# A two-layer hybrid decoder trunk: the engines' order laid out against another machine model

## Chip, core and metric
The kernel runs on one core of a Trainium2 chip. The metric is the device time of one execution in microseconds; the time given is the median of three runs. A profiled execution of the same program gives the rows below.

## The reference, cut to what matters
Two layers, each with a token mixer, a cross-attention and a feed-forward block, every one between two RMSNorms. All data is fp32; x is 512 x 1024.

```python
for l in range(DEPTH):                                   # DEPTH = 2
    a = hybrid_mixer(rms_norm(x, pre_mix_g[l]), positions, rel_bias, w_in[l], ...)
    x = x + rms_norm(a, post_mix_g[l])
    c = memory_cross_attention(rms_norm(x, pre_xattn_g[l]), rms_norm(mem, mem_g[l]), ...)
    x = x + rms_norm(c, post_xattn_g[l])
    hdn = square(relu(rms_norm(x, pre_mlp_g[l]) @ w_up[l]))
    x = x + rms_norm(hdn @ w_down[l], post_mlp_g[l])
# hybrid_mixer: z = h @ w_in is split into latent columns (8 heads of latent attention, causal,
# keys and queries through low-rank w_ukv and w_uq with rotary columns) and q, k, v of 8 dilated
# heads (three dilations with a shared relative bias, merged by their softmax denominators);
# both groups side by side @ w_mix_out
```

## The kernel before
The kernel is written in a tile framework: the source calls engine operations on tiles from pools, and the framework works out the waits, the buffers and the order of each engine's stream. Rows of x lie in four tiles of 128 tokens.

Every large product is made of three fp32r matmuls. A weight chunk `raw` (two blocks of 128 rows by up to 512 columns, loaded by SP, 8 buffers) is split into `whi` by ACT (L142, L162 or L167, the last with the norm's gain) and `wlo = raw - whi` by DVE (L143, L163, L172), 5 buffers each; x and other left sides are split likewise (L176 and L178). `mm` (L204 to L213) then adds high x low, low x high and high x high into one PSUM bank. `tok_major_steps` and `feat_major_steps` run such products with tokens or features on the partitions and write the PSUM tiles `ptm` and `pfm`.

The mixer is the one stage with two strands. `attention()` goes through 16 heads, first the eight dilated ones, then the eight latent ones. For each: the score matmuls `sp` (L432, two PSUM banks), DVE's `tensor_tensor_reduce` (L436), which adds the bias or mask table, writes `P` and the row's extreme `nm`, ACT's exponential (L438), DVE's reciprocal (L439), POOL's scaling (L440), the transposes `ptp` (L198) with their copies `PT` by ACT (L459) or DVE (L457), and for every two heads the product with the values `op` (L202). A dilated head takes a table `tb` of bias and log counts of its own, loaded by SP (L640). The other strand, `latent()` and `memory()`, are the latent projections and the keys and values of the cross-attention; `weave` calls steps of it between steps of attention, by a ratio of the PE time that both strands take by a count in the source:

```python
weave(attention(), [latent_gen, memory()], lambda: RATIOS[0] if not scored[0] else RATIOS[1])
```

A norm (`norm_x`) takes ACT's squares `junk` (L344), DVE's mean `n1m` (L348), POOL's power `n1r` (L124), POOL's scaled rows `xn` (L375) and eight PE transposes `tp` (L198). At the end of a feed-forward block `done` (sum of squares, product with the gain, L994) and `add_post_norm` (`pnr`, `xs`, L387 to L390) come before it. The feed-forward block makes `w_down`'s product from seven sub-products per quarter (L1020 to L1049); the partial sums are added into `acc` on DVE (L1047, L1049).

The order of the streams: the source gives a sequence for all engines together. On leaving the `with` block at L1093 the framework plays the program against a model of the machine. Each instruction that the model holds to be ready, with its buffer free, is taken in the order of the source; one that isn't ready is passed by. What comes out is the order that each engine then keeps on the chip: the queues of PE, DVE, ACT, POOL and SP are run in order. All 384 DMAs are issued by SP.

## Time and profile before
| | |
|---|---|
| median of three runs | 1551.03 us (1550.02 to 1554.45) |
| profiled execution | 1552.36 us, its span 1550.6 us |
| mean granted TensorE clock | 0.992 |
| PE busy | 1504.3 us, 97% of the span |
| PE weight loads (PEld) | 1263.1 us, 81% |
| DVE busy | 993.8 us, 64% |
| ACT busy | 819.0 us, 53% |
| POOL busy | 240.7 us, 16% |

The span runs from the first to the last instruction. The granted clock is a share of full speed, 2.4 GHz; the lower level is 1.2 GHz. On the time axis the first mixer's two-strand part lies at about 86 to 265 us, the first feed-forward block at about 500 to 773, the second layer's mixer at about 851 to 1030 and its feed-forward block at about 1270 to 1540. Idle time is told with what ended it; a wait of a matmul counts where PE had nothing else in its queue.

### The profile page before, as it was taken

The numbers are of one execution on the slowest core, as the hardware profiler recorded it, in microseconds if no ns is written. First come the engines' busy times: TensorE is split into PE (matmuls) and PEld (weight loads), VectorE is DVE, ScalarE is ACT, GpSimd is POOL, SyncE is SP. The second block draws the span as 40 slices with busy tenths as digits, with TensorE's granted clock in tenths as the row PEclk, the third lists the DMA queues.
The fourth block names the chain that finished last, engine by engine and source line by source line (L and its number), as shares of the span: only waits on it lengthen the run. The fifth ranks groups of instructions, "written<-read, shape, count | busy, mean of one in ns | idle before, by whom it ended". The sixth has DMA issues, their size and how long they took to land.

```text
span 1550.6 us, 21224 instructions
## 1 busy us (share of the span) xinstructions
PE 1504.3 (97%) x7831; PEld 1263.1 (81%) x7831; DVE 993.8 (64%) x1775; ACT 819.0 (53%) x1574; POOL 240.7 (16%) x433
## 2 busy tenths in 40 slices
PE   7999999999999999999999899999999999999997
PEld 5777788898898888888778877878988988888885
DVE  4655766456458677686954558663654595867678
ACT  5455766345356364545644557653553654636363
POOL 2033621021020000000022346211120200000000
PEclk9999999999999999999999999999999999999998
DMA  6432223514131505151631322234322325060522
GB/s 225 153 116 68 89 69 102 197 55 123 55 109 55 176 28 185 33 176 42 219 106 49 115 75 96 69 123 163 107 71 77 113 60 173 14 190 21 184 69 81
DMA packets 87403, 164.07 MB, mean 106 GB/s; under 512 B 6230, under 2 KB 12036, under 8 KB 87300
## 3 DMA queue, kind: packets, MB, share of 16 engines
q1 hardware_dynamic: 87300, 162.73, 32.7%
q8 instruction: 61, 1.00, 0.3%
q14 instruction: 42, 0.34, 0.1%
HBM read 154.29 MB, written 11.03 MB: 107 GB/s over the span
## 4 chain that ended last, share of the span: by engine, by line
PE 83%; DVE 7%; issue 4%; ACT 2%; POOL 2%; DMA 2%; SPq 0%; DVEq 0%; POOLq 0%; ACTq 0%
PE pfm L212 12%; PE pfm L211 12%; PE pfm L213 12%; PE ptm L211 6%; PE ptm L212 6%; PE ptm L213 6%; PE wa L211 3%; PE wa L212 3%; PE wa L213 3%; PE sp L432 3%; PE op L202 3%; DVE wlo L172 2%; PE ptp L198 2%; PE wc L211 2%; PE wc L212 2%
## 5 line engine op out<-in xcount | busy, mean ns | idle before, releaser
L212 PE MATMUL pfm<-xth,wlo 128*128 128x512 f32 (+1 forms) x896 | 322.4, 360 | 0.6
L211 PE MATMUL pfm<-xtl,whi 128*128 128x512 f32 (+1 forms) x896 | 322.2, 360 | 0.0
L213 PE MATMUL pfm<-xth,whi 128*128 128x512 f32 (+1 forms) x896 | 321.6, 359 | 0.0
L172 DVE SCALAR_TENSOR_TENSOR wlo<-raw,gT,whi 128x512 fp32r<-128x512 f32 (+3 forms) x332 | 229.5, 731 | 132.7 <-ACT whi L167 131.1
L167 ACT ACTIVATE whi<-raw,gT 128x512 fp32r<-128x512 f32 (+2 forms) x324 | 208.9, 697 | 177.8 <-PE pfm L213 92.7
L142 ACT ACTIVATE whi<-raw 128x1024 fp32r<-128x1024 f32 x112 | 118.9, 1061 | 139.8 <-PE pfm L213 52.8
L212 PEld LDWEIGHTS pfm<-xth,wlo 128*128 128x128 f32 x896 | 169.3, 189 | 26.9 <-DVE wlo L172 1.4
L213 PEld LDWEIGHTS pfm<-xth,whi 128*128 128x128 f32 x896 | 169.2, 189 | 25.6 <-issue 0.5
L211 PEld LDWEIGHTS pfm<-xtl,whi 128*128 128x128 f32 x896 | 169.3, 189 | 24.8
L143 DVE TENSOR_TENSOR wlo<-raw,whi 128x1024 fp32r<-128x1024 f32 x112 | 134.8, 1220 | 32.0 <-ACT whi L142 32.0
L124 POOL TENSOR_TENSOR pnr<-pnm,mhalf 128x1 f32<-128x1 f32 x24 | 16.1, 672 | 828.3 <-DVE pnm L387 828.3
L211 PE MATMUL wa<-wlo,fh 128*128 128x512 f32 x256 | 99.8, 390 | 0.5 <-DVE acc L1047 0.5
L212 PE MATMUL wa<-whi,fl 128*128 128x512 f32 x256 | 99.6, 389 | 0.0
L213 PE MATMUL wa<-whi,fh 128*128 128x512 f32 x256 | 99.6, 389 | 0.0
L440 POOL TENSOR_SCALAR P<-P,rs 128x128 f32<-128x128 f32 (+3 forms) x128 | 71.1, 560 | 152.3 <-DVE rs L439 79.3
L438 ACT ACTIVATE P<-P,nm 128x128 f32<-128x128 f32 (+3 forms) x128 | 71.1, 557 | 32.9 <-DVE nm L436 32.1
L163 DVE TENSOR_TENSOR wlo<-raw,whi 128x1024 fp32r<-128x1024 f32 x32 | 39.1, 1223 | 59.3 <-ACT whi L162 58.6
L211 PE MATMUL ptm<-wlo,xth 128*128 128x512 f32 (+2 forms) x192 | 69.4, 362 | 1.8 <-ACT xth L176 1.8
L162 ACT ACTIVATE whi<-raw 128x1024 fp32r<-128x1024 f32 x32 | 34.0, 1061 | 67.3 <-PE ptm L213 64.5
L212 PE MATMUL ptm<-whi,xtl 128*128 128x512 f32 (+2 forms) x192 | 68.5, 357 | 0.4 <-DVE xtl L178 0.4
L213 PE MATMUL ptm<-whi,xth 128*128 128x512 f32 (+2 forms) x192 | 67.2, 350 | 0.0
L211 PEld LDWEIGHTS wa<-wlo,fh 128*128 128x128 f32 x256 | 48.0, 188 | 11.3 <-DVE acc L1047 1.4
(244 smaller groups left out, 3254.0 us busy)
## 6 DMA issues: line engine op xcount, KB each, us to landing
raw<-in_w_up SPq DMA_DIRECT2D x64, 512.0 KB, 4.7
raw<-in_w_down SPq DMA_DIRECT2D x64, 512.0 KB, 4.4
raw<-in_w_in SPq DMA_DIRECT2D x24, 512.0 KB, 7.0
raw<-in_w_xk SPq DMA_DIRECT2D x16, 512.0 KB, 4.2
raw<-in_w_xv SPq DMA_DIRECT2D x16, 512.0 KB, 3.8
raw<-in_w_mix_out SPq DMA_DIRECT2D x16, 512.0 KB, 4.2
raw<-in_w_xq SPq DMA_DIRECT2D x16, 512.0 KB, 6.0
raw<-in_w_xo SPq DMA_DIRECT2D x16, 512.0 KB, 3.6
```

Source lines behind the costliest of these rows:

```text
L142: nc.scalar.activation(hi, raw, AF.Copy)
L143: nc.vector.tensor_sub(lo, raw, hi.bitcast(F32))
L163: nc.vector.tensor_sub(lo[:, :kts, :width], raw[:, :kts, :width], hi[:, :kts, :width].bitcast(F32))
L167: nc.scalar.activation(cols(hi, k, False), cols(raw, k, True), AF.Copy, scale=g)
L172: nc.vector.scalar_tensor_tensor(lv, rv, g, hv, op0=OP.mult, op1=OP.subtract)
L202: nc.tensor.matmul(ps, lhsT=lhsT, rhs=rhs, start=start, stop=stop)
L211: nc.tensor.matmul(ps, lhsT=lh, rhs=rl, start=first, stop=False, skip_group_check=more)
L212: nc.tensor.matmul(ps, lhsT=ll, rhs=rh, start=False, stop=False, skip_group_check=more)
L213: nc.tensor.matmul(ps, lhsT=lh, rhs=rh, start=False, stop=last, skip_group_check=more)
L432: nc.tensor.matmul(sp[:, :L], lhsT=q[:, i * 128:(i + 1) * 128], rhs=k[:, :L], start=n == 0, stop=n == len(parts) - 1)
L438: nc.scalar.activation(Pi, Pi, AF.Exp, bias=nm[:, i:i + 1], scale=-1.0, accum_out=rs[:, i:i + 1])
L440: nc.gpsimd.tensor_scalar(Pi, Pi, rs[:, i:i + 1], 1.0, op0=OP.mult, op1=OP.mult)
```

## The change
One argument of the framework's context is set, so that the model against which the order is laid out is another one of the framework's, a simulator of the timeline that has its own prices for operations, waits and transfers. The source of the work is the same.

```diff
-    with tile.TileContext(nc) as tc:
+    with tile.TileContext(nc, schedule_with_timeline_sim=True) as tc:
         block_kernel(tc, *args, o)
```

## Rows read from the trace of the kernel before

**Rows 1.** The page's first part: busy us (share of the span), instructions.
```profile
PE 1504.3 (97%) x7831; PEld 1263.1 (81%) x7831; DVE 993.8 (64%) x1775; ACT 819.0 (53%) x1574; POOL 240.7 (16%) x433
```

**Rows 2.** Busy time by stretch (columns in the first line).
```profile
core 0: us, PE busy (x) PEld busy (x) DVE busy (x) ACT busy (x) POOL busy (x), PEclk, DMA share, GB/s
0.00:30.00 30.00, 20.07 (x84) 15.05 (x84) 13.52 (x23) 16.50 (x35) 10.19 (x21) 1.00 0.82 290
...
90.00:110.00 20.00, 17.26 (x103) 14.28 (x102) 8.80 (x28) 11.23 (x29) 2.91 (x6) 0.91 0.41 135
...
140.00:150.00 10.00, 7.09 (x43) 4.72 (x41) 7.09 (x22) 6.39 (x17) 3.12 (x5) 1.00 0.67 231
150.00:200.00 50.00, 47.23 (x284) 38.16 (x283) 39.95 (x115) 34.33 (x88) 33.63 (x66) 1.00 0.25 79
...
500.00:770.00 270.00, 269.75 (x1190) 223.03 (x1190) 200.26 (x256) 141.49 (x204) 0.00 (x0) 1.00 0.38 121
770.00:800.00 30.00, 24.38 (x111) 18.40 (x110) 20.19 (x38) 14.91 (x35) 13.09 (x16) 0.94 0.42 133
...
850.00:870.00 20.00, 17.90 (x115) 16.68 (x115) 11.42 (x42) 10.93 (x33) 7.58 (x13) 0.91 0.32 107
870.00:900.00 30.00, 28.09 (x173) 24.28 (x171) 15.92 (x52) 16.11 (x45) 8.95 (x21) 0.94 0.28 88
900.00:915.00 15.00, 11.82 (x63) 10.19 (x62) 9.98 (x27) 9.52 (x21) 4.19 (x13) 0.89 0.53 175
915.00:965.00 50.00, 47.18 (x283) 38.07 (x282) 38.77 (x112) 33.63 (x87) 33.57 (x66) 1.00 0.25 80
...
1540.00:1551.00 11.00, 0.15 (x1) 0.00 (x0) 6.39 (x12) 1.34 (x4) 1.48 (x2) 0.60 0.42 157
```

**Rows 3.** Waits of PE: who waited for whom, us in total, times, longest.
```profile
PE sp L432 <- DVE nm L436: 12.2, 11, 2.0
PE tp L198 <- POOL xn L375: 10.8, 6, 4.9
...
PE ptp L198 <- ACT PT L459: 2.3, 4, 0.8
```

**Rows 4.** Timeline, 84 to 102 us: start, us, engine, what, [idle before <-releaser].
```profile
88.25 0.28 PE L432 MATMUL sp<-kh,qs 128*128 128x256 f32 x1
...
97.43 3.15 ACT L167 ACTIVATE whi<-raw,gT 128x384 fp32r<-128x384 f32 x6 [8.49 <-issue]
...
98.08 1.15 DVE L172 SCALAR_TENSOR_TENSOR wlo<-raw,gT,whi 128x384 fp32r<-128x384 f32 x2 [8.28 <-ACT whi L167]
...
101.22 0.28 DVE L436 CUSTOM_DVE_ANT_0 P<-sp,tb 128x128 f32<-128x128 f32 x1
```

**Rows 5.** Timeline of SP's queue, 825 to 890 us.
```profile
832.21 18.15 SPq L135 DMA_DIRECT2D raw<-in_w_uq  x2
...
852.21 0.41 SPq L640 DMA_DIRECT2D tb<-tabw  x1
```

**Rows 6.** Timeline, 855.9 to 859.2 us.
```profile
856.10 0.30 PE L212 MATMUL ptm<-whi,xtl 128*128 128x288 f32 x1
858.09 0.29 DVE L436 CUSTOM_DVE_ANT_0 P<-sp,tb 128x128 f32<-128x128 f32 x1 [2.64 <-DMA tb<-tabw]
...
858.44 0.44 PE L432 MATMUL sp<-kh,qs 128*128 128x384 f32 x1 [2.04 <-DVE nm L436]
```

**Rows 7.** Timeline of DVE, 764 to 796 us.
```profile
773.32 0.69 DVE L1049 TENSOR_TENSOR acc<-wa,acc 128x512 f32<-128x512 f32 x1
773.92 0.15 DVE L348 SCALAR_TENSOR_TENSOR n1m<-n1ms 128x1 f32<-128x1 f32 x1
```

**Rows 8.** All on the tile tb: DVE's waits for it, issue to landing.
```profile
  DMA tb<-tabw: 10.7, 4
...
DMA to landing us min/median/max: 2.6/4.6/6.0
```

## Prediction

> **What bounds the kernel now.** I read the page's busy times first, then the busy time by stretch, then who waits for whom on PE, then the timelines around PE's largest stops. PE is the bound: 1504.3 us of 1550.6 are busy, while DVE has 64% and ACT 53% [rows 1]. So the time is PE's own work, which this change leaves as it is, plus PE's stops, 46.3 us, plus what PE loses at the lower of its two clock levels (1.2 instead of 2.4 GHz).
>
> Where the 46.3 us lie is read from the stretches [rows 2]: 9.9 in the first 30 us, where the first rows of x and the first weights are on their way; 10.9 behind the last matmul, where the last norm and the stores run; 5.6 between the layers (770 to 800 us); and in the two mixers 18.4, as 2.74 + 2.91 + 2.77 in the first and 2.10 + 1.91 + 3.18 + 2.82 in the second. In a feed-forward stage PE is busy for 269.75 of 270 us. Those stages have nothing to gain.
>
> A stop costs more than itself. In five of the stretches with such stops the granted clock reads 0.89 to 0.94 and not 1.00 [rows 2]. Length times what is missing to 1: 20 x 0.09 + 20 x 0.09 + 30 x 0.06 + 15 x 0.11 = 7.05 us in the mixers, and 30 x 0.06 = 1.8 between the layers. So the mixers hold 18.4 + 7.05 = 25.5 us that an order of instructions could change, the joint of the layers 7.4.
>
> Who ends these stops: 12.2 of PE's idle time, in 11 waits, is a score matmul `sp` (L432) that waits for DVE's `nm` (L436), which frees one of the two score banks; 10.8 is a transpose that waits for POOL's `xn` (L375) [rows 3]. The latter fall in the start and the joint, the former all in the mixers.
>
> **The change part by part.** Not one operation, shape or wait of the source changes. The framework lays out each engine's stream by running the program against a model of the machine, and among what the model calls ready it takes what stands first in the source; the flag replaces the model. So the edit is a new order on five in-order queues (PE, DVE, ACT, POOL, and SP, which issues all the DMAs), and other waits where buffers now change hands in another order. Neither can be read from the trace; what can be read is where the order of before does not suit the chip.
>
> DVE's order, first mixer. Head 0's scores were in PSUM at 88.4 us (`sp` at 88.25, 0.28 long), yet DVE reduced them from 101.22 on. Its queue held two `wlo` (L172) ahead, and they waited 8.28 us for ACT's `whi`, which itself stood 8.49 us [rows 4]. The model had taken this weight split to be ready early, and on the chip it was not. PE had fill work for most of it and stopped for 1.9 to 2 us only, plus the clock's 1.8.
>
> SP's order, second mixer. SP stood before the second `raw` of w_uq from about 832.6 to 850, the pair covering 18.15 us, and head 0's bias table `tb` (L640) was issued behind it, at 852.21 [rows 5]. DVE then waited 2.64 us for it, and PE stopped from 856.4 to 858.44, 2.04 us [rows 6]. DVE had four such waits for tables, 10.7 us in all; tables take 2.6 to 6.0 us to land, half of them over 4.6 [rows 8].
>
> What a better fitting order is worth: the score stops with their clock loss come to 12.2 + 7.05 = 19.2 us. The bounds are nothing and all of it. I take half, 9.6, because two causes that an order can cure are seen at these stops (a split ahead of the reduction on DVE, a weight load ahead of the table on SP), while the third, that the next head's chain of reduction, exponential, scaling and transpose is simply long, stays. Against it I set two new stops of the size of PE's waits for `PT`, 2.3 us in 4 waits, 0.6 each [rows 3]: with 0.2 for each in lost clock, 1.6. Net: -8.0.
>
> The joint of the layers: the chain of add, norm, `pnr`, `xs`, squares, `n1r`, `xn`, transpose is fixed by data; an order can take DVE's `acc` of 0.69 us out from before `n1m` [rows 7], or put one more there. Bounds -2 and +2, taken at 0. The start: SP's loads of x and of the first weights share one queue; bounds -2 and +3, taken at 0, because a greedy order has few choices before the data lands. The tail: 0, within 1. The feed-forward stages and the projections: 0, since PE's idle time there is 0.25 of 270 us with DVE busy for 200 of them [rows 2], so that a split of 1 us made later stays hidden; if that cover is gone, rival C prices it. In the program as built before, 1397 of PE's 7701 matmuls stand at another place than in the source, and none in the feed-forward stages but their first group; so there is little order to change there.
>
> The sum: the profiled run took 1552.36 us (span 1550.6 and 1.8 around it); 1552.36 - 8.0 = 1544.4. The median of the runs shown is 1.33 below the profiled run, so the forecast for a median is 1543 us.
>
> One rule that reads the room otherwise. The kernel's PE is 97% busy, and its weight loads 81% [rows 1]. The Trainium skill (Perfetto Trace Analysis, Identifying the Most-Contended Engine) calls matmul busy time a bad measure of how near TensorE is to its limit, and names the share of LDWEIGHTS as the better one; by it 19% of the span would be room, some 290 us as an estimate. The trace speaks against it here: in the feed-forward stage without stops the weight loads stand at 223 of 270 us, 83%, hardly above the whole kernel's share, so this share is what the pace itself looks like. I leave it as rival D.
>
> **The rivals.**
> A, no change that can be measured: the stops move and their sum stays. For it: half of the 46.3 us (start, tail, joint) hang on chains of data, and PE's work is the same. Price: 0, so 1551, with 1546.4 to 1555.7 as its bounds; 0.3%, 4.7 us, is about what a measurement of this kernel tells from no change. Chance 0.26.
> B, slower through SP's queue: the new order puts weight loads that wait for a `raw` buffer ahead of more tables. It decides at the table's lead: a table that is issued less than its 4.6 to 6.0 us ahead of its first reduction stops DVE, and behind it PE [rows 6, 8]. A stop of that kind costs 2.04 and 1.8 of clock, 3.84 us. Of 16 tables 4 were late before. If four more are, it is + 15.4: 1566 us. For it: SP stood 18 us before one load already, and the source fixes how much fill PE gets between two steps of attention, so that steps which DVE and ACT now take in another order meet the same fill. Against it: the tables stand ahead of the weights in the source, so a model that gets buffer release right takes them first. Chance 0.24.
> C, slower in the feed-forward stages: a late `wlo` there has no fill work on PE. At one stall of about 1.2 us in each of the eight quarters it is + 10: 1561 us. Against it: PE waited nowhere in them before. Chance 0.04.
> D, the room of the page's rule: PE's matmuls come closer together. If an order took out every stop in the mixers and the joint (25.5 + 7.4) it would be 1518 us; the pace between stops does not depend on order in any row. Chance 0.02.
> That the flag does nothing belongs to A.
>
> **How the numbers follow.** Faster as forecast 0.44 (1543; its own range 1532 to 1546, from the score stops all gone, with 2 at the joint, down to just measurable); A 0.26; B 0.24; C 0.04; D 0.02. Faster 0.46, same 0.26, slower 0.28. The range of 8 in 10 goes from 1531, where the forecast's bounds end, to 1566, which leaves out the worse half of B and D.
>
> **What would show it.** Right: PE's waits for `nm` fall from 12.2 us to about half, the granted clock in the mixers' stretches rises to 0.95 or more, DVE's waits for `tb` nearly vanish, and the reduction of head 0 follows its scores within a few us. The stretch of a feed-forward stage keeps its 270 us of work. Wrong: DVE's waits for `tb` above 10.7 us (B); PE idle in a feed-forward stage by more than 2 us (C); mixers with the same idle sum at other places (A); or a start or joint that moves by more than 3 us, which I have at 0. The weakest step is the half of 19.2: it is a choice between bounds, not a measurement.

## The result

The changed kernel takes 1594.35 us in the median of four runs (1592.73 to 1594.75), the kernel before 1552.62 in four runs beside it (the 1551.03 told ahead is the median of three of them). The ratio is 1.0272, 95% interval [1.0249, 1.0295]: slower by some 42 us, where the forecast was 1543 and its range ended at 1566.

The profiled execution has a span of 1593.0 us, 42.4 more than before, at a mean granted clock of 0.987 (0.992 before). The page's first part answers to [rows 1]:

```profile
PE 1523.2 (96%) x7831; PEld 1267.3 (80%) x7831; DVE 991.5 (62%) x1775; ACT 812.8 (51%) x1574; POOL 248.4 (16%) x433
```

PE is busy 18.9 us longer with the same 7831 instructions, and idle 69.8 us instead of 46.3. To see where, the span is cut at these matmuls: the first scores, the first matmul of the mixer's output projection, the first and the last matmul of the down projections, the first scores of the second layer and so on. The stretch from the last down projection to the next scores is called the joint. Busy time by these stretches up to the end of the second mixer, first the kernel before, then the changed one (length, then PE, PEld, DVE, ACT, POOL busy; third from the right the granted clock):

```profile
0.00:86.50 86.50, 76.57 (x328) 59.91 (x329) 44.95 (x93) 40.18 (x75) 17.89 (x33) 1.00 0.49 170
86.50:278.30 191.80, 182.85 (x1146) 152.18 (x1145) 121.86 (x347) 119.74 (x287) 68.31 (x136) 0.99 0.30 94
278.30:489.80 211.50, 211.22 (x1201) 184.72 (x1200) 117.78 (x188) 103.93 (x214) 31.05 (x48) 1.00 0.32 102
489.80:773.00 283.20, 282.95 (x1248) 233.97 (x1248) 211.13 (x271) 151.55 (x220) 0.99 (x1) 1.00 0.37 117
773.00:851.20 78.20, 72.58 (x323) 58.31 (x323) 41.78 (x70) 33.97 (x66) 19.80 (x27) 0.98 0.27 81
851.20:1045.00 193.80, 183.51 (x1146) 155.27 (x1145) 123.23 (x347) 118.04 (x286) 68.59 (x136) 0.97 0.30 95
```

```profile
0.00:97.40 97.40, 81.27 (x327) 62.89 (x328) 43.91 (x92) 40.42 (x75) 17.13 (x33) 0.95 0.44 150
97.40:296.80 199.40, 188.39 (x1146) 153.68 (x1145) 123.23 (x347) 119.51 (x288) 76.69 (x136) 0.98 0.30 97
296.80:513.70 216.90, 211.99 (x1200) 184.31 (x1201) 116.48 (x187) 102.40 (x213) 28.11 (x48) 1.00 0.29 95
513.70:798.30 284.60, 282.95 (x1248) 233.97 (x1247) 210.97 (x272) 148.59 (x217) 0.50 (x1) 1.00 0.37 116
798.30:880.90 82.60, 72.99 (x323) 59.34 (x322) 42.09 (x71) 35.17 (x69) 17.99 (x28) 0.94 0.26 80
880.90:1082.10 201.20, 190.18 (x1146) 154.74 (x1144) 122.88 (x347) 118.20 (x287) 77.00 (x136) 0.97 0.29 96
```

The start grew by 10.9 us, the mixers by 7.6 and 7.4, the stretch from output projection to the end of cross-attention by 5.4 (5.5 in the second layer), the feed-forward stage by 1.4 in each layer, the joint by 4.4; the tail is 1.5 shorter. Only in the mixers did PE's busy time grow much, by 5.5 and 6.7 us. The start's 4.7 more stand beside a clock of 0.95. Over the whole span the lower clock, length times what is missing to 1, comes to 1593.0 x 0.013 = 20.7 us instead of 1550.6 x 0.008 = 12.4.

Who ends PE's idle time now, the rows that answer to [rows 3] (total us, times, longest):

```profile
PE tp L198 <- POOL xn L375: 14.4, 3, 6.2
PE pfm L211 <- DVE xtl L178: 7.8, 4, 1.9
PE ptm L211 <- DVE otl L178: 5.9, 4, 2.2
PE ptp L198 <- DVE mtl L178: 5.7, 4, 2.3
PE ptp L198 <- POOL P L440: 5.0, 6, 1.4
...
PE sp L432 <- DVE nm L436: 1.2, 2, 0.6
```

The stops on which the forecast rested are gone: scores waiting for `nm` fell from 12.2 us to 1.2. In their place stand stops for pieces that were hardly late before, none of them over 0.5 us in total: the halves of activations (`xtl`, `otl`, `mtl`) and scaled scores (`P`). Those for the norm's rows (`xn`) grew from 10.8 us to 14.4. In the mixers PE's idle time went from 8.95 + 10.29 = 19.2 us to 11.01 + 11.02 = 22.0.

### The profile page after: what moved, and what is told of

Its sections match the earlier page's. It is cut to its first block, busy times and chain, and to the rows that moved or that the text cites. A ratio compares the mean times of both kernels' runs of the same rounds, so it can differ in the third digit from the quotient of the medians.

```text
span 1593.0 us, 21212 instructions
## 1 busy us (share of the span) xinstructions
PE 1523.2 (96%) x7831; PEld 1267.3 (80%) x7831; DVE 991.5 (62%) x1775; ACT 812.8 (51%) x1574; POOL 248.4 (16%) x433
## 4 chain that ended last, share of the span: by engine, by line
PE 86%; DVE 6%; issue 3%; POOL 3%; ACT 2%; DMA 0%; DVEq 0%; SPq 0%; POOLq 0%; ACTq 0%
PE pfm L211 12%; PE pfm L213 12%; PE pfm L212 12%; PE ptm L211 7%; PE ptm L212 6%; PE ptm L213 6%; PE wa L211 3%; PE wa L213 3%; PE wa L212 3%; PE op L202 3%; PE sp L432 3%; PE ptp L198 2%; PE wc L212 2%; PE wc L211 2%; DVE wlo L172 2%
## 5 line engine op out<-in xcount | busy, mean ns | idle before, releaser
L142 ACT ACTIVATE whi<-raw 128x1024 fp32r<-128x1024 f32 x112 | 118.0, 1060 | 135.9 <-PE wa L213 54.3
L440 POOL TENSOR_SCALAR P<-P,rs 128x128 f32<-128x128 f32 (+3 forms) x128 | 87.8, 691 | 160.7 <-DVE rs L439 154.5
L459 ACT ACTIVATE PT<-ptp 128x512 f32<-128x512 f32 x64 | 34.5, 540 | 71.2 <-PE ptp L198 51.1
L198 PE MATMUL ptp<-ident,P 128*128 128x128 f32 x320 | 55.9, 282 | 12.3 <-DVE mtl L178 5.7
```

The lines of the kernel that those rows point to most:

```text
L142: nc.scalar.activation(hi, raw, AF.Copy)
L198: nc.tensor.transpose(out_, in_, ident_)
L440: nc.gpsimd.tensor_scalar(Pi, Pi, rs[:, i:i + 1], 1.0, op0=OP.mult, op1=OP.mult)
```

## Experiments

The two layouts were crossed. A helper queues the instructions of one engine, or of one engine in one stretch, in an order recorded from the other kernel; the edges fix the order of issue and add no wait. What a run does not queue is laid out around it by the base's model.

```diff
+def _pin(nc, tc, packed):
...
+            if prev is not None:
+                tc.add_manual_dep(by[name], prev, _mb.DependencyInfo(
+                    _mb.DependencyClass.NoSync, _mb.DependencyReason.DATA), reason="pin")
...
         block_kernel(tc, *args, o)
+        _pin(nc, tc, _ORDER)
```

Two bases are used: "changed" has the flag set, "before" has not; `_ORDER` holds what each run says. In the traces of e10, e12 and e14 to e17 nothing stands elsewhere but what is named and, in e10 and e16, a single load. On the changed base more moves than is named: in e4 and e8 some 330 matmuls of each mixer stand elsewhere than in the changed kernel. The eight value matmuls `op` of a head pair are called an eight, or a group. The results together, as ratio to the kernel before on the same chip with its 95% interval; beside it, from the trace, how much longer than before the stretches of the profiled execution are (start, first and second mixer, the two stretches of projections and cross-attention, the two feed-forward stages, joint; the tail, between 1.6 us less and no change, is left out). It is cut at the exact starts of the matmuls, so that some figures differ by 0.1 us from those above.

| run | ratio | start | mixers | proj. + cross-att. | ff | joint |
|---|---|---|---|---|---|---|
| changed kernel | 1.0272 [1.0249, 1.0295] | 11.0 | 7.5, 7.4 | 5.4, 5.5 | 1.4, 1.4 | 4.4 |
| e1 PE's order of before, in the changed | 1.0229 [1.0207, 1.0251] | 5.7 | 6.0, 3.3 | 4.8, 4.8 | 5.8, 5.9 | 0.8 |
| e2 PE's order of the changed, in before | 1.0269 [1.0245, 1.0293] | 3.8 | 14.6, 10.8 | 4.4, 6.0 | 0.8, 0.8 | 0.1 |
| e4 start as before, in the changed | 1.0198 [1.0175, 1.0220] | 0.0 | 7.9, 5.7 | 6.9, 6.9 | 1.4, 1.4 | 4.4 |
| e8 the same, SP alone | 1.0212 [1.0192, 1.0232] | 2.6 | 6.4, 5.7 | 7.0, 6.9 | 1.4, 1.4 | 4.4 |
| e16 start: SP as changed, in before | 1.0060 [1.0043, 1.0078] | 10.3 | 5.0, -4.0 | -0.1, -0.1 | 0.0, 0.0 | 0.4 |
| e3 projections as before, in the changed | 1.0210 [1.0189, 1.0230] | 9.8 | 7.7, 7.0 | 0.6, 0.6 | 1.4, 1.4 | 6.0 |
| e7 the same, PE alone | 1.0247 [1.0230, 1.0264] | 9.6 | 7.5, 7.0 | 3.7, 3.7 | 1.4, 1.4 | 6.0 |
| e9 the same, DVE and ACT alone | 1.0262 [1.0242, 1.0281] | 11.0 | 9.3, 6.4 | 3.3, 3.1 | 1.4, 1.4 | 4.4 |
| e14 projections: DVE, ACT as changed, in before | 1.0118 [1.0099, 1.0136] | 0.3 | 4.9, -2.1 | 7.1, 8.7 | 0.0, 0.0 | 0.5 |
| e15 projections: PE as changed, in before | 1.0050 [1.0036, 1.0065] | 0.2 | 1.3, -5.1 | 5.2, 4.8 | 0.0, -0.1 | 0.5 |
| e11 ff and joint as before, in the changed | 1.0194 [1.0179, 1.0209] | 8.4 | 7.2, 3.2 | 6.4, 4.8 | 0.0, 0.0 | 0.2 |
| e17 joint: DVE, ACT as changed, in before | 1.0048 [1.0033, 1.0063] | -0.7 | 1.1, -2.5 | 0.0, 0.0 | 1.3, 0.0 | 7.6 |
| e10 mixers as changed, in before | 1.0087 [1.0070, 1.0104] | 0.0 | 8.4, 5.1 | 0.0, -0.1 | 0.0, 0.0 | 0.7 |
| e12 eights broken, in before | 1.0174 [1.0157, 1.0191] | -0.2 | 15.2, 13.8 | 0.0, -0.1 | 0.0, 0.2 | 0.4 |
| e6 eights whole, in before | 1.0008 [0.9996, 1.0021] | -1.6 | 4.5, -3.7 | 0.0, 0.0 | 0.0, 0.0 | 0.5 |
| e13 the same, second layer alone | 1.0013 [1.0001, 1.0024] | -0.5 | 1.2, -0.1 | -0.1, 0.0 | 0.0, 0.0 | 0.0 |
| e5 eights whole, in the changed | 1.0244 [1.0226, 1.0261] | 8.3 | 6.4, 5.2 | 6.8, 6.8 | 1.4, 1.4 | 4.4 |

A mixer is not to be read finer than some 5 us from one profile: in the runs e14 to e17, whose mixers have the order of before, they read from 5.1 us less to 5.0 us more. The start of the changed kernel, in the same order on all queues in e3, e5, e7, e9 and e11, reads 8.3 to 11.0 us, and its first stretch of projections, unmoved in e4, e5 and e8, 6.8 to 7.0 where the changed kernel has 5.4. The second mixer of the profile of before ran at a granted clock of 0.97, that of e16 at 0.99.

### One engine's order throughout: e1 and e2

In e1 the flag is set and PE is queued as before; in e2 it is not set and PE is queued as in the changed kernel.

> The schedule is laid out as in the changed kernel, but PE's 7701 matmuls are queued in the order that they have in the kernel before; the other four engines' orders are laid out anew around that. Theory 1 (the loss is in PE's order: PE reaches transposes and sums later than their data are ready, and stops at the seams): the 42 us go, time 1548 to 1558 us, PE idle back to 44 to 52 us. Theory 2 (the loss is in the other queues: DVE, ACT, POOL and SP put the pieces that PE waits for behind other work): 1580 to 1598 us, and the stops for xtl, otl and mtl stay. Between 1562 and 1578 both have a part.


Measured: 1588.63 us (1587.33 to 1590.95).


> The converse: the schedule is laid out as in the kernel before, but PE's matmuls are queued in the order of the changed kernel. Theory 1 (PE's order): 1586 to 1600 us, with the stops of PE for xtl (8 us in 4), otl (6 us in 4) and mtl back, and those for nm near 1 us. Theory 2 (the other queues): 1550 to 1562 us.


Measured: 1594.67 us (1593.73 to 1595.87).

By the time, theory 1 fits e2 and fails on e1, theory 2 the other way round: neither holds alone. With PE's old order the other engines, laid out by the new model around it, lose elsewhere: in the feed-forward stages 5.8 us each, where the changed kernel loses 1.4, and PE stands 7.3 us for `acc`. So the loss can't be put down to one queue of the whole program; it has to be looked for stretch by stretch.

### The start: e4, e8 and e16

> Laid out as in the changed kernel, but up to the end of the first in-projection (before the first scores) all engines' instructions, SP's loads among them, keep the order of the kernel before. Theory A (the loss belongs to the stretch): the 11 us of the start come back, 1581 to 1586 us, and the scores start at the time of the kernel before within 1 us. Theory B (the first scores wait for something else, such as the tables): under 4 us, 1590 to 1595 us.


Measured: 1584.51 us (1581.28 to 1585.64), the scores at the time of the kernel before. Theory A holds: 1.0272 falls to 1.0198, 11 us.

> As the changed kernel, but up to the first scores SP's loads alone keep the order of the kernel before (there the loads of xs come ahead of seven of the weights'). Theory L (the start's 11 us are late loads): as with all engines' order put back, 1582 to 1586 us. Theory E (the engines' orders lose it, the loads only a part): the stop of 3.4 us for xn near 26 us goes, and little more: 1588 to 1593 us.


Measured: 1586.70 us (1585.31 to 1587.00), 9 of the 11 given back, just above the range of theory L. It is not the loads alone: 83 of the start's matmuls stand elsewhere too, laid out around them. The next run moves loads only.

> The kernel before with nothing moved but 15 loads on SP's queue ahead of the first scores, which stand as in the changed kernel (the loads of the third and fourth tile of x, xs, behind six loads of w_in instead of between them); all engines keep the order of the kernel before. Theory L (the start's 11 us are these late rows): 7 to 11 us, 1560 to 1564. Theory E (the rows cost the one stop of 3.4 us and the rest is the engines' order): 1555 to 1557.


Measured: 1561.51 us (1559.34 to 1563.88) where the kernel before takes 1551.57: theory L. Fifteen loads in other places, and nothing else, cost 9 to 10 us. The timeline of SP's queue, before and changed, shows which (start, time on the queue; x2 and so on counts loads in a row; in e16 one of the eight loads of w_in stands between the third and the fourth tile):

```profile
5.17 1.23 SPq L94 DMA_DIRECT2D xs<-in_x  x2
...
8.50 1.71 SPq L135 DMA_DIRECT2D raw<-in_w_in  x2
11.19 1.72 SPq L94 DMA_DIRECT2D xs<-in_x  x2
12.96 1.46 SPq L135 DMA_DIRECT2D raw<-in_w_in  x3
14.46 1.23 SPq L94 DMA_DIRECT2D xs<-in_x  x2
```

```profile
6.84 1.64 SPq L94 DMA_DIRECT2D xs<-in_x  x2
9.42 7.98 SPq L135 DMA_DIRECT2D raw<-in_w_in  x8
17.53 4.41 SPq L94 DMA_DIRECT2D xs<-in_x  x4
```

The third and fourth tile of x are issued at 11.19 and 14.46 us before and from 17.53 on in the changed kernel, behind eight loads of w_in in a row. PE then waits for the late rows. First its stop in the changed kernel, then its two in e16:

```profile
30.11 1.97 PE L198 MATMUL tp<-ident,xn 128*128 128x128 f32 x8 [3.25 <-POOL xn L375]
```

```profile
18.64 0.69 PE L198 MATMUL tp<-ident,xn 128*128 128x128 f32 x2 [3.28 <-POOL xn L375]
...
28.78 0.79 PE L211 MATMUL ptm<-wlo,xth 128*128 128x512 f32 x1 [3.62 <-ACT xth L176]
```

Over the start PE stands 16.1 us in the changed kernel and 15.4 in e16 instead of 9.9, and its clock reads 0.95 and 0.93 instead of 1.00, with 4.7 us more of busy time in both.

### Projections and cross-attention: e3, e7, e9, e14 and e15

> Laid out as in the changed kernel, but in the stretches from the mixer's output projection to the end of cross-attention, in both layers, all engines' instructions keep the order of the kernel before. Theory A (each loss belongs to the order of the stretch in which it shows): the 11.5 us that these stretches lost come back and nothing else, 1581 to 1585 us. Theory B (the losses of a stretch are carried in from the one ahead of it, or what is won is lost at the next seam): under 4 us come back, 1590 to 1595 us.


Measured: 1585.79 us (1584.53 to 1587.24), 9 to 10 us less than the changed kernel; in the trace each of the two stretches is back to 0.6 us above before. The time is just above the range of theory A; theory B is out.

> As the changed kernel, but in the stretches from the mixers' output projections to the end of cross-attention PE alone keeps the order of the kernel before; DVE, ACT, POOL and SP stay as laid out by the other model. Theory 1 (in these stretches the loss is made by PE's order, which takes the norm's transposes later): as with all engines' order put back, 1584 to 1588 us, and no stop at the first projection after either. Theory 2 (DVE and ACT have put weight splits between the steps of the norm): the transposes wait for xn instead, 1590 to 1597 us.


Measured: 1591.69 us (1591.22 to 1592.94).


> As the changed kernel, but in the stretches from the mixers' output projections to the end of cross-attention DVE and ACT keep the order of the kernel before (so that no weight split stands between two steps of a norm that did not stand there before); PE is laid out by the other model around that. Theory 2 (there the loss is made by the splits between the norm's steps): as with all engines' order put back, 1584 to 1588 us, and the stops for xtl at the next projection (7.8 us in 4) gone. Theory 1 (it is made by PE's order, whose part alone measured 2.9 us): 1590 to 1595 us.


Measured: 1592.97 us (1589.53 to 1596.18).


> The kernel before with nothing moved but DVE and ACT instructions of the stretches from the mixers' output projections to the end of cross-attention, which take the order of the changed kernel (133 of DVE's, 76 of ACT's stand elsewhere); PE, POOL and SP keep the order of the kernel before in full. These stretches grew by 5.4 and 5.5 us in the changed kernel. Theory S (the loss is made by weight splits that stand between the norm's steps on DVE and ACT): 8 to 12 us, 1561 to 1565. Theory P (it is made by PE, whose transposes of the norm stand 10 to 11 matmuls later): under 3 us, 1552 to 1556.


Measured: 1571.03 us (1566.93 to 1572.95).


> The counterpart: the kernel before with nothing moved but PE's matmuls of the same stretches, which take the order of the changed kernel; DVE, ACT, POOL and SP keep the order of the kernel before in full. Theory P: 8 to 12 us, 1561 to 1565. Theory S: 2 to 4 us, 1555 to 1557, as PE's order alone gave back 2.9 us in the changed kernel. If both this run and its counterpart lose most of the 11 us, each order fits only its own partner.


Measured: 1560.13 us (1559.41 to 1560.47).

Put back alone, either side leaves more than half of the loss (7.4 us of 10.9 with PE's order back, 6.4 with DVE's and ACT's). Brought alone into the kernel before, either side makes it: DVE and ACT 15.8 us, more than both together, PE 10.0. Both theories were too simple: e7 lies in the range of theory 2 and e9 in that of theory 1, which can't both hold, and e14 and e15 lie in neither range. The orders of the engines in a stretch are one plan: here half of it without the other half cost about as much as all of the bad plan or more.

What the plan does is seen at the end of the norm ahead of a projection. The timeline of before, then of the changed kernel, from the transposes of its last needed tile to the first matmul behind:

```profile
320.01 1.03 PE L198 MATMUL tp<-ident,xn 128*128 128x128 f32 x8
...
321.83 1.06 ACT L176 ACTIVATE xth<-tp 128x512 fp32r<-128x512 f32 x2
...
322.44 1.29 DVE L178 TENSOR_TENSOR xtl<-tp,xth 128x512 fp32r<-128x512 f32 x2
...
323.61 0.28 PE L211 MATMUL pfm<-xtl,whi 128*128 128x256 f32 x1
```

```profile
340.18 3.40 DVE L172 SCALAR_TENSOR_TENSOR wlo<-raw,gT,whi 128x512 fp32r<-128x512 f32 x5
...
340.64 1.32 ACT L167 ACTIVATE whi<-raw,gT 128x512 fp32r<-128x512 f32 x2
340.86 1.04 PE L198 MATMUL tp<-ident,xn 128*128 128x128 f32 x8
...
342.48 1.05 ACT L176 ACTIVATE xth<-tp 128x512 fp32r<-128x512 f32 x2
...
343.56 1.28 DVE L178 TENSOR_TENSOR xtl<-tp,xth 128x512 fp32r<-128x512 f32 x2
...
344.30 0.39 PE L211 MATMUL pfm<-xtl,whi 128*128 128x256 f32 x1 [1.94 <-DVE xtl L178]
```

From transposes to the first matmul it is about as long in both, 3.60 and 3.44 us. Before, PE fills it with matmuls of the output projection. In the changed kernel these transposes stand 10 to 11 matmuls later in PE's queue, past that fill, only two matmuls are left behind them, and PE stops for 1.94 us. Meanwhile DVE and ACT have weight splits (`wlo`, `whi`) queued between the steps of the norm. There are four such stops for `xtl`, 7.8 us, two in each layer; the stretch lost 5.4.

### Feed-forward and joint: e11 and e17

> As the changed kernel, but in the feed-forward stages and at the joint of the layers all engines keep the order of the kernel before. Theory A (each loss belongs to its stretch): the 4.4 us of the joint, 2 us of the feed-forward stages and the 1.8 us stop in each come back: 1586 to 1590 us. Theory B (what is won is lost at the next seam): 1592 to 1597 us.


Measured: 1581.97 us (1580.98 to 1584.59). That is 12 us less than the changed kernel, above what theory A expected: the stretches themselves gave back 4.2 + 2.8. The rest does not lie in them: the start, in the order of the changed kernel, reads 2.6 us shorter in this profile, and the second mixer, where 338 matmuls stand elsewhere than in the changed kernel, 4.2.

> The kernel before with nothing moved but 71 DVE and 26 ACT instructions from the first layer's last quarter of the feed-forward to the end of the joint, which stand as in the changed kernel (two additions of the last wa ahead of the xs of the first two tiles, and weight splits between); PE, POOL and SP keep the order of the kernel before. Theory S (the joint's 4.4 us come from what DVE and ACT put ahead of the norm's steps): 3 to 6 us, 1556 to 1559. Theory P (they come from PE's order at the joint): within 1.5 us of the kernel before.


Measured: 1559.48 us (1557.44 to 1561.50): theory S, with more than the 3 to 6 us: the joint alone grew by 7.6, where the full plan costs 4.4. That PE's queue no longer fits would explain it; PE's order at the joint was not run by itself. The timeline of the changed kernel at the joint:

```profile
797.80 0.55 POOL L124 TENSOR_TENSOR pnr<-pnm,mhalf 128x1 f32<-128x1 f32 x1 [321.93 <-DVE pnm L387]
798.24 0.74 DVE L172 SCALAR_TENSOR_TENSOR wlo<-raw,gT,whi 128x512 fp32r<-128x512 f32 x1
798.89 0.68 DVE L1049 TENSOR_TENSOR acc<-wa,acc 128x512 f32<-128x512 f32 x1
799.50 0.74 DVE L172 SCALAR_TENSOR_TENSOR wlo<-raw,gT,whi 128x512 fp32r<-128x512 f32 x1
800.15 1.41 DVE L390 SCALAR_TENSOR_TENSOR xs<-acc,pnr,xs 128x512 f32<-128x512 f32 x2
...
804.90 0.47 PE L198 MATMUL tp<-ident,xn 128*128 128x128 f32 x1 [6.20 <-POOL xn L375]
```

The factor `pnr` is ready at 798.35. The `xs` that needs it stands on DVE behind two splits and the addition of the last `wa`, until 800.15: 1.8 us on the chain that PE waits for. The chain is late besides: `xs` begins 1.8 us behind the start of the block's last matmul (the cut at 798.3), where before it began 1.7 us ahead of it (the cut at 773.0):

```profile
771.32 1.42 DVE L390 SCALAR_TENSOR_TENSOR xs<-acc,pnr,xs 128x512 f32<-128x512 f32 x2 [0.44 <-POOL pnr L124]
```

In the kernel before, that addition came behind `xs`, ahead of `n1m` [rows 7].

### The mixers: e10, e12, e5, e6 and e13

> The kernel before, but in the two mixers (from the first scores to the last head pair's values) all engines keep the order of the changed kernel. Theory A (the mixers lose by their own order: op broken into pieces, 16 us more of PE's time, against 11 us of stops for nm that go): the 15 us by which the mixers grew in the changed kernel, 1564 to 1572 us. Theory C (their growth is carried in from what was late before them; by its own order a mixer wins what the stops for nm gave): 1543 to 1552 us.


Measured: 1566.07 us (1565.29 to 1566.45), 13.5 us more than before: theory A, with the losses of its own order. The waits for `nm` are at 1.4 us in this run too, those for `P` at 7.4 and for `mtl` at 4.5; PE's idle time in the two mixers is 20.6 us against 19.2. What grew is PE's time in the eight value matmuls of a head pair, `op`. Their busy time in the whole program, from busy time by stretch for this tile alone, before and changed:

```profile
sum 1600.00, PE 45.87 PEld 20.00 DVE 11.05 ACT 9.55; mean PE 22.94 PEld 10.00 DVE 5.53 ACT 4.78
```

```profile
sum 1600.00, PE 59.54 PEld 20.34 DVE 11.02 ACT 9.45; mean PE 29.77 PEld 10.17 DVE 5.51 ACT 4.72
```

The same 128 matmuls, recorded as 256, take 13.7 us longer. (Counted from a piece's start to that of the next matmul, stops left out, it is 44.1 and 56.0 us, 11.9 more; the expectations count so, and the 60.4 in one of them has 4.4 us of stops in it.) A step's two matmuls, one per head, fill 64 columns of PE each; in the trace their records start 6 to 7 ns apart when they stand next to each other. Where the eight lie in one piece (before, first fence) they take 2.38 us; cut by other matmuls (run e12, second fence) 1.07 + 1.72 + 0.86 = 3.65:

```profile
227.76 2.38 PE L202 MATMUL op<-PT,vm 128*64 128x512 f32 x16
```

```profile
257.35 1.07 PE L202 MATMUL op<-PT,vm 128*64 128x512 f32 x2
...
259.93 1.72 PE L202 MATMUL op<-PT,vm 128*64 128x512 f32 x8
...
263.16 0.86 PE L202 MATMUL op<-PT,vm 128*64 128x256 f32 x6
```

The kernel before had 9 of 16 groups in one piece; the changed one has none, each is cut into three or four. Where only the first matmul stood apart, as in five groups before, a group took 3.44. The Trainium skill (TensorEngine Tiling (Array Packing), Key Properties) says that the tiles of a split array work independently and in parallel, and that a change of the tiling mode drains the engine. The trace agrees with the first: side by side within a group, and more time where a cut parts a pair. No run here shows a drain by itself.

Three runs asked what this time is worth. In e12 the groups of the kernel before are cut and no other engine is touched (chains for all five engines, PE's with the fill matmuls moved). In e5 and e6 the first of the eight waits for the last of the pair's transposes (e6: order only) or for their last eviction (e5):

```diff
-                mm32(op[e * 64:(e + 1) * 64, j * 128:512], v_of(e, j), PTs[e][j], ...)
+                o = mm32(op[e * 64:(e + 1) * 64, j * 128:512], v_of(e, j), PTs[e][j], ...)
+                if j == 0:
+                    tc.add_manual_dep(o.ins, last_ptp[0].ins.name, mybir.DependencyInfo(
+                        mybir.DependencyClass.NoSync, mybir.DependencyReason.DATA), reason="whole")
```

In e13 the condition also asks for the second layer. In e5 13 of the 16 groups came out whole, in e6 all, and the layout moves some of DVE's and ACT's instructions besides.

> As the changed kernel, but the first of the eight value matmuls of a head pair (op, L469) also waits for the last eviction of the pair's transposes, so that 14 of the 16 groups of eight lie in one piece on PE (the changed kernel splits each into three or four pieces, the kernel before splits 7 of 16). Theory P (a broken group costs PE time of its own, since the two heads' matmuls of a step run side by side only when they stand next to each other: 60.4 us of op in the changed kernel, 44.1 in the kernel before, 2.30 us for a whole group): op falls to 37 us and the time to 1571 to 1578 us. Theory Q (the time of op only stands where PE would otherwise stop, or a later op delays otl): 1588 to 1597 us.


Measured: 1591.63 us (1589.74 to 1592.36), `op` at 39.7 us.


> As the kernel before, but the first of the eight value matmuls (op, L469) is queued on PE behind the last transpose of its head pair, so that all 16 groups lie in one piece (7 are in two or three pieces before). Theory P: op falls from 44.1 to 37 us, the time by 5 to 8 us, to 1545 to 1548 us where the kernel before takes 1552.8. Theory Q (what op gives back is lost in stops for later pieces): within 2 us of the kernel before.


Measured: 1554.41 us (1551.41 to 1560.03), `op` at 38.8 us: the same as before.


> The kernel before with nothing moved but PE matmuls of the fill: each of the 16 groups of eight value matmuls (op) is cut between its fifth and sixth by six fill matmuls that stood behind it, and the nine whole ones also between the first and second; DVE, ACT, POOL and SP keep the order of the kernel before in full. Theory P (broken groups cost the mixers their own time): op rises from 44.1 us to 53 to 56 us, as in the changed kernel's mixers run alone (55.6), and the time by 8 to 12 us, to 1560 to 1565: then most of the 13.4 us of those mixers is this. Theory Q (op's longer time lies in stops that are there anyway, as making the groups whole gave nothing): op rises as much, the time to 1552 to 1556 us, and the mixers' loss is in the order of the other engines' pieces (P, mtl, PT).


Measured: 1579.17 us (1578.58 to 1581.90), `op` at 59.6 us.


> The kernel before, but in the second layer alone the first of the eight value matmuls is queued on PE behind the last transpose of its head pair, so that the eight groups there lie in one piece. In the run with this in both layers the first layer's mixer took 4.5 us more (a longer stop near 99 us, with the granted clock at 0.64 in 100 to 110 us) and the second layer's 3.6 us less. Theory G (whole groups win where no stop and no clock loss follows): 1547.5 to 1550.5 us where the kernel before takes 1552.6. Theory Q (they win nothing; what differed was where the clock fell in one profiled run): 1551.5 to 1554 us.


Measured: 1554.46 us (1552.98 to 1558.77).

Theory P fails on e5 and e6, and theory G on e13: whole groups took 7 us of `op` away in e6 and 20 in e5, and the time fell by nothing in e6 and in e5 by some 4, within the intervals of the two ratios. The sums over both mixers, before and in e6 (all us):

```profile
sum 385.60, PE 366.37 PEld 307.45 DVE 245.09 ACT 237.78 POOL 136.90; mean PE 183.18 PEld 153.73 DVE 122.54 ACT 118.89 POOL 68.45
```

```profile
sum 386.50, PE 362.82 PEld 305.77 DVE 245.99 ACT 237.73 POOL 137.50; mean PE 181.41 PEld 152.88 DVE 122.99 ACT 118.87 POOL 68.75
```

Of the 7.0 us, 4.2 went into stops for `nm` (16.4 us instead of 12.2). PE's busy time fell by 3.6 only, beside a clock of 0.96 in the first mixer instead of 0.99. In e5 the stops for `nm` rose from 1.2 us to 8.8. In e12 the loss was larger than theory P allowed: 13.8 us more in `op`, and PE's idle time in the mixers 29.1 us instead of 19.2, with `nm` at 19.9. So, as far as these runs show, the early first matmul of a group lies in a stop that is there anyway and costs nothing, while a group cut behind its fifth matmul holds up the chain of the attention strand and costs more than its own time; e12 cuts nine groups behind their first matmul as well, and the two cuts were not run apart. What the cuts cost inside the changed kernel's own mixers is not settled: there they also fill stops, and making the groups whole gave some 4 us, no more than the intervals leave open.

The four parts measured by themselves, start 9.3 (e16), projections 9.6 (e3), feed-forward and joint 12.1 (e11), mixers 13.5 (e10), come to 44.5 us by the ratios; the changed kernel lost 42.2. That the two come so close is in part luck: each figure is good to some 3 to 5 us, e3 and e11 move other instructions too, and some 5 of the 12.1 do not lie in the stretches that e11 puts back. What is shown is that each stretch lost by an order of its own, since each of the four parts was moved in one kernel or the other and its loss came or went with it. No combination tried here beats the kernel before.

## Why the prediction was wrong

**The score stops.** Right in kind, and more than forecast: 12.2 fell to 1.2, not to a half. DVE's waits for `tb` fell from 10.7 us in 4 to 4.0 in 2, and the reduction of head 0 follows its scores by 5.9 us (97.4 to 103.3) instead of 13.0. What failed is the price set against it, two new stops of 0.8 us. The idle time of the mixers rose by 2.8, under other names: `P`, `mtl`, `otl`. That is the mechanism of rival A. Nor did the clock's part of the 19.2 come back: it reads 0.99 and 0.97 over the two mixers before, 0.98 and 0.97 after.

**"PE's own work, which this change leaves as it is."** This was the step that hid the most in the mixers. PE's work has the same instructions and not the same time: `op` took 13.7 us more, because its pairs were pulled apart. What that is worth in the time of the mixers stays open. The time of a pair could have been read in the trace of before, where whole and cut groups stand beside each other.

**The start, 0 within -2 and +3.** It moved by 10.9, and 15 loads on SP's queue alone by 9.3. The reason given, that a greedy order has few choices before the data lands, failed: a load of x waits for no result, so it can change places, and four tiles of x share the queue with the weights. Rival B had the right queue and the wrong place, tables in the mixers, and a price of 15.4.

**The projections, 0.** The step read the cover from the feed-forward stage, 0.25 us idle of 270, and carried it to the projections, which have a norm ahead of them. They lost 5.4 and 5.5. The feed-forward stages themselves lost 1.4 each, so for them the 0 was nearly right, and rival C's late piece showed up a stage earlier. That 1397 matmuls stood elsewhere than in the source was no measure either: between the two kernels 4285 of PE's 7701 matmuls change place, some 1000 of them between the first and the last down projection of a layer, where they cost 1.4 us each time.

**The joint, 0 within 2.** It lost 4.4. The step named the right thing, an `acc` put in front, but it stands in front of `xs` and with two splits beside it, 1.8 us on the chain instead of 0.69; how the rest divides was not measured.

**The range.** Its lower end is given as 1532 and as 1531, while its terms, 1551 - 19.2 - 2, make 1530; the upper end is what failed, by 28 us. Each zero had its bound, but the rivals moved one thing at a time. A new order moves all five queues in every stage at once. The forecast added the one gain that the trace showed and left the losses at zero, because a good order leaves no row that shows what a worse one would cost. PE busy for all of a stretch says that this order fits there; it does not say that another would.

**The page's rule (rival D).** The Trainium skill (Perfetto Trace Analysis, Identifying the Most-Contended Engine) warns that matmul busy time is a bad measure. It names two measures in its place, the matmul work done against the peak and the share of the weight loads; the prediction used only the second. The warning held here in a way I had not used: PE's busy time rose by 18.9 us on the same work, while the weight loads went from 1263.1 to 1267.3. The 19% of room that the prediction read from the second measure shows in no run.

## What to carry to other kernels

A change of the order of a tuned program is a change of every stage at once: cost each stage where a chain of small steps ends (a norm ahead of a projection, the first rows at the start, the joint), by what stands between its steps on each in-order queue, and not by how full the bound engine looks now. PE's time depends on the order where two matmuls share the array, so count whole and cut groups. To find where an order loses, queue one stretch, then one engine of it, in the other kernel's order; expect that half of a plan can cost as much as all of it.

## What the hardware showed that I had not expected

Eight value matmuls of 64 columns take 2.38 us in one piece and 3.65 us in three pieces, both at a granted clock of 1.00. Fifteen loads of the first 25 us, moved among themselves, cost 9.3 us: PE stood 15.4 us over the start instead of 9.9, and its granted clock was 0.93 there instead of 1.00. And the 7.0 us that a faster `op` gave came back as waits for `nm` (12.2 to 16.4 us) and as PE's other work at a lower clock: with PE busy for 95% of the mixers (366.4 of 385.6 us), a shorter `op` did not shorten them.
